# Products of 512 columns in place of two of 256 in some steps of a gated-linear-attention block

## The chip, the cores and the metric

The kernel runs on one core of one Trainium2 chip. The metric is device time in microseconds of one execution, taken as the median over several runs. A profile is one further execution, recorded by the hardware profiler; its span goes from the first to the last instruction of the program, and its own time is a little longer than that.

The core has a matrix engine (TensorE, in the profile PE; its loads of the stationary operand are listed apart as PEld), a vector engine (VectorE, DVE), a scalar engine (ScalarE, ACT), GpSimd (POOL) and SyncE (SP), which issues most of the DMAs. TensorE reads its operands from on-chip memory (SBUF) and adds its products into eight banks of accumulators (PSUM), each of 128 partitions by 512 float32.

## The reference

One layer of a hybrid encoder: 256 tokens, width 2048, depth 1, so that the only mixer is gated linear attention (GLA), followed by a squared-ReLU MLP and a final normalization. Everything is float32.

```python
def reference(x, ...):
    h = x
    h = h + _gla_mixer(_rmsnorm(h, gla_norm), gla_w_in, gla_w_gate_up, gla_b_gate, gla_o_norm, gla_w_out)
    h = h + _sq_relu_mlp(_rmsnorm(h, mlp_norm), mlp_w_up, mlp_w_down)
    return _rmsnorm(h, final_norm)

def _gla_mixer(h, w_in, w_gate_up, b_gate, o_norm, w_out):
    q, k, v, r, g_low = split(h @ w_in)          # 1024, 1024, 2048, 2048, 16 columns
    log_a = log_sigmoid(g_low @ w_gate_up + b_gate) / 16
    # four heads, chunks of 64 tokens: a decayed state per head, read by q
    ...
    return (normalized(o) * silu(r)) @ w_out

def _sq_relu_mlp(h, w_up, w_down):               # 2048 -> 8192 -> 2048
    a = relu(h @ w_up)
    return (a * a) @ w_down
```

## The kernel before

**Precision.** Each float32 matrix is split into a high and a low part that the matrix engine takes in one pass each (type `F32R`): `hi` is a rounded copy, made by ScalarE (line 109), `lo` the difference, made by VectorE (line 110). A product of two matrices A and B is three products: high by high, high by low, low by high. A weight tile of 128 rows and up to 1040 columns is loaded into `raw` by SyncE's DMA queue (line 132, function `weights`) and then split into a slot of the rings `hi` and `lo`, five slots each. `raw` has three buffers, each of which holds two tiles.

**The two forms of a projection.** In `natural` the tokens are the stationary operand, in blocks of 128 tokens by 128 inputs, and the weight columns move through TensorE; the output has tokens on partitions. It makes 16 steps over the 2048 inputs (`kt`). In each step there are two token blocks `t`, three terms, and the parts of the output's columns given by `cuts`; `HALF` is two parts of 512, each one PSUM bank. The part of 512 columns is issued by the helper `halves` (line 140) as products of `T` = 256 columns each, with the same stationary operand, one after the other. A width that isn't a multiple of 256 is issued whole: the first stage has a part of 272 columns, that is three products of 256 and one of 272 for each token block and term. In `turned` (line 169) the weights are the stationary operand and the 256 tokens move, so that each product has 256 columns.

**Stages, in order.** First half of the values with the gate's low-rank input (`w_vg`); keys and queries (`turned`, two halves of 512 outputs each); second half of the values (`3 * KEYW`, with the steps in the order `late`); two gate projections (`4 * KEYW` and `5 * KEYW`, 1024 columns each), after each of which `gate_out` applies the SiLU and multiplies with the attention's output; two output projections (`w_out`, 1024 columns each) with the attention's output, transposed, as the stationary operand (`row_o`); then four rounds of the MLP, each of four `up` passes (`turned`, 512 hidden units each) and a `down` pass for each half of the output's columns. The last half of the last round is written out apart, with the final normalization.

**The down pass.** `down(r, half, act)` makes an output of 256 tokens by 1024 columns from 2048 hidden units. For the first 512 of its columns it uses a Strassen-like scheme over pairs of steps (banks `b32`, `b74`, `b16`, `b50`; combined weights are made by VectorE in `work`). The other 512 columns, the plain half, are ordinary products: `blocks`, for both token blocks and three terms, into the two banks `plain`. In the first pair of steps (`PLAIN`) everything is ordinary.

**Addresses.** The stationary operands of the projections lie at chosen places of SBUF. The normalized input `xth`, `xtl` has rows of 320 elements at an offset of 48; for step `EVEN` = 5 a copy in the tile `xe` is used instead. The output projection's operand (`row_o`, line 528) has the offset 48 before step 5, 64 at step 5, and 112 after it. In `turned` the weight slots have the offset 48, or 0 in the steps that `even` names.

**Order of the work.** Small pieces of other work wait in the list `side` and are issued by `pump`, one after each step: scores, attention (`attend`, itself with products of 256 columns through `halves`), transposes (`turn`, line 515), sums of squares. The order on each engine is then settled by a planner that simulates a timeline as the program is built; so products of neighbouring steps and of side work can be found interleaved in the trace. TensorE's queue carries nothing but products and transposes.

Of the kernel before, what the change touches and what calls it, by code (L numbers as in the profile page):

```python
# [34 lines left out]
NT = T // P  # L35
D = 2048
KT = D // P
# [3 lines left out]
KEYW = HEADS * DK  # L41
# [5 lines left out]
G = 1024  # L47
# [19 lines left out]
def tile_gla_mlp(ctx, tc, x, xt, cols, w_vg, w_in, w_gate, w_out, w_up, w_down, final_norm, out):  # L67
    nc = tc.nc
# [10 lines left out]
    def acc_banks(n):  # L79
        return [acc_p.tile([P, 512], F32, tag="acc", name="acc") for _ in range(n)]  # L80
# [7 lines left out]
    def pump(n=1):  # L88

        with tc.issue_after(last_hi[0].ins), tc.issue_after(last_lo[0].ins):  # L90
            for _ in range(n):
                if side:
                    side.popleft()()

    def flush():
        while side:
            side.popleft()()
# [4 lines left out]
    def slots(off=0):  # L102
        return [wpool.tile([P, SLOT], F32R, tag=i, name=i)[:, off:] for i in ("hi", "lo")]

    def parts(raw, n, to, pieces=None):

        hi, lo = to
        for s in (slice(*p) for p in pieces or [(0, n)]):
            last_hi[0] = nc.scalar.copy(hi[:, s], raw[:, s])  # L109
            last_lo[0] = nc.vector.tensor_tensor(lo[:, s], raw[:, s], hi[:, s].bitcast(F32), op=ALU.subtract)  # L110
        return hi, lo
# [3 lines left out]
    def raw_pair():  # L115
        a = wpool.tile([P, 2 * WMAX], F32, tag="raw", name="raw", bufs=3)
        return a[:, :WMAX], a[:, WMAX:]

    def weights(src, n, pieces=None, room=None, skip=0, raw=None, off=0):

        to = room or slots(off)
        if raw is None:
            if not raw_half:
                raw_half.extend(raw_pair())
            raw = raw_half.pop(0)
        for s in (slice(*p) for p in pieces or [(0, n)]):
            dst = raw[:, s]
            if len(src.shape) == 3:
                dst = dst.rearrange("p (i c) -> p i c", i=2)
                last_load[0] = nc.sync.dma_start(out=dst, in_=src)  # L130
            else:
                last_load[0] = nc.sync.dma_start(out=dst, in_=src[:, s])  # L132
        return parts(raw, n, to, pieces or [(skip, n)])

    def halves(o, x, w, first, last):

        n = w.shape[-1]
        for c in range(0, n, T) if n % T == 0 else (0,):
            m = slice(c, c + T) if n % T == 0 else slice(0, n)
            nc.tensor.matmul(o[:, m], x, w[:, m], start=first and c == 0, stop=last, skip_group_check=True)  # L140

    def natural(row, source, n, cuts, pumps=1, ahead=None, order=range(KT)):

        acc = acc_banks(NT * len(cuts))
        acc = [acc[t * len(cuts) : (t + 1) * len(cuts)] for t in range(NT)]
        for step, kt in enumerate(order):
            wh, wl = weights(source(kt), n, ahead and ahead(kt))
            for t in range(NT):
                sh, sl = (a[:, t * P : (t + 1) * P] for a in row(kt))
                for i, (s, w) in enumerate(((sh, wh), (sh, wl), (sl, wh))):  # L150
                    for c, (lo, hi) in enumerate(cuts):
                        halves(acc[t][c], s, w[:, lo:hi], step == 0 and i == 0, step == KT - 1 and i == 2)
            if step < KT - 1:
                pump(pumps)
        return acc
# [21 lines left out]
    HALF = [(0, 512), (512, 1024)]  # L177

    def rows(w, c0, n=G, r0=0):
        return lambda kt: w[r0 + kt * P : r0 + (kt + 1) * P, c0 : c0 + n]  # L180
# [50 lines left out]
    cuts = [(0, 512), (512, 768), (768, WMAX)]  # L231
# [80 lines left out]
    acc = natural(row_x, rows(w_vg, 0, WMAX), WMAX, cuts, ahead=input_tile)  # L312
# [92 lines left out]
    for half in range(2):  # L405
        acc = turned(*xts, w_in, KEYW + half * GT, even=(0,) if half else (2,))
# [18 lines left out]
    for half in range(2):  # L425
        acc = turned(*xts, w_in, half * GT, even=())
# [6 lines left out]
    at = big.tile([P, 2, HEADS, 3 * P + 64], F32R, tag="C", name="at")  # L433
# [36 lines left out]
    acc = natural(row_x, rows(w_in, 3 * KEYW), G, HALF, order=late)  # L470
# [49 lines left out]
            nc.scalar.activation(dh, s, AF.Copy, scale=gain(kt))  # L520
            nc.vector.scalar_tensor_tensor(dl, s, gain(kt), dh.bitcast(F32), op0=ALU.mult, op1=ALU.subtract)

    acc = natural(row_x, rows(w_in, 4 * KEYW), G, HALF)
    flush()
    gate_out(acc, 0)
    oth, otl = (big.tile([P, KT * T + 128], F32R, tag="B", name="ot" + i) for i in "hl")
# [7 lines left out]
    acc = natural(row_x, rows(w_in, 5 * KEYW), G, HALF)  # L534
# [20 lines left out]
    acc = natural(row_o, rows(w_out, 0), G, HALF)  # L555
# [3 lines left out]
    row_h = lambda kt: [a[:, kt, :] for a in (hth, htl)]  # L559
    side.extend([lambda: None] + [lambda q=q: turn(h, row_h, g2, q) for q in range(4)])  # L560
    side.append(lambda: ssq_h(0))
    acc = natural(row_o, rows(w_out, G), G, HALF)
    flush()
    add_h(acc, G)
    side.extend([lambda q=q: turn(h, row_h, g2, q) for q in range(4, 8)])
# [24 lines left out]
    A11, A12, A21, A22, S3, S1, S2, S4 = range(8)  # L590
# [35 lines left out]
    def down(r, half, act):  # L626

        c0 = half * G
        plain = [aux_bank(), aux_bank()] if half == 0 else acc_banks(2)
        b32, b74 = acc_banks(2) if half == 0 else [aux_bank(), aux_bank()]  # L630
        b16, b50 = acc_banks(2)
        left, right = slice(0, T), slice(T, 2 * T)
        used = set()

        def product(bank, o, a, w, m, last):

            for i, (x, y) in enumerate(((0, 0), (0, 1), (1, 0))):
                halves(bank[:, o], a[x], w[y][:, m], bank.name not in used, last and i == 2)
                used.add(bank.name)

        for kp in range(KP):
            last = kp == KP - 1
            at = lambda f: stationary(act, kp, f)
            w = rows(w_down, c0, G, r * D)
            blocks = lambda i, wi: [
                product(plain[t], slice(0, 512), at((A11, A21)[t] + i), wi, slice(512, G), last and i == 1) for t in range(NT)
            ]
            if kp in PLAIN:
                for i in range(2):
                    wi = weights(w(2 * kp + i), G)  # L650
                    blocks(i, wi)
                    product(b32, slice(0, 512), at(A11 + i), wi, slice(0, 512), False)
                    product(b50, right, at(A21 + i), wi, left, False)
                    product(b74, right, at(A21 + i), wi, right, False)
                    pump()
                continue
            assert not raw_half
            pair = wpool.tile([P, 2 * WMAX], F32, tag="raw", name="raw", bufs=3)
            raw0, raw1 = pair[:, :WMAX], pair[:, WMAX:]
            w0 = weights(w(2 * kp), G, skip=T, raw=raw0)  # L660
            product(b16, left, at(A11), w0, right, last)
            blocks(0, w0)
            pump()
            w1 = weights(w(2 * kp + 1), G, raw=raw1)
            u = work[:, kp % 2].rearrange("p (f s) -> p f s", f=4)
            add = lambda o, x, y: nc.vector.tensor_tensor(o, x, y, op=ALU.add)

            both = pair[:, T : T + 2 * (WMAX - T)].rearrange("p (k c) -> p k c", k=2)[:, :, :T]
            add(u[:, :2], raw0[:, left].unsqueeze(1).to_broadcast([P, 2, T]), both)
            add(u[:, 2], u[:, 0], raw1[:, left])  # L670
            add(u[:, 3], u[:, 2], raw1[:, right])
            wu = parts(work[:, kp % 2], G, slots())
            product(b32, right, at(A12), w1, right, last)
            product(b32, left, at(S4), w1, left, last)
            blocks(1, w1)
            product(b50, left, at(S1), wu, slice(0, T), last)
            product(b74, left, at(S3), wu, slice(T, 2 * T), last)
            product(b16, right, at(S2), wu, slice(2 * T, 3 * T), last)
            product(b74, right, at(A22), wu, slice(3 * T, G), last)
            if not last:  # L680
                pump()
        flush()
        for t in range(NT):
            take(plain[t], t, c0 + 512, 512)

        tt = lambda o, x, y: nc.vector.tensor_tensor(o, x, y, op=ALU.subtract)
        nc.scalar.copy(ends[:, 1], b16[:, left])
        tt(ends[:, 3], ends[:, 1], b16[:, right])
        tt(ends[:, 0], b50[:, left], ends[:, 3])
        tt(ends[:, 2], ends[:, 3], b74[:, left])  # L690
        take(b32, 0, c0, 512)
        take(b74, 1, c0, 512)
        take(b50[:, right], 1, c0, T)
        for t in range(NT):
            hv = h[:, t, c0 : c0 + 512].rearrange("p (i s) -> p i s", i=2)
            nc.vector.tensor_tensor(hv, hv, ends[:, 0 : t + 2 : t + 1], op=ALU.add)
# [23 lines left out]
    cuts = [HALF, [(0, 512), (512, 768), (768, 1024)]]  # L720
    acc = [acc_banks(len(cuts[t])) for t in range(NT)]
# [10 lines left out]
    for kt in range(KT):  # L732
        k = kt - KT + ROOM
        w = weights(rows(w_down, G, G, (ROUNDS - 1) * D)(kt), G, room=k >= 0 and [room[:, i, k, :] for i in range(2)])
# [68 lines left out]
```

## Time and profile before

| | us |
|---|---|
| Median of 3 runs | 1075.46 (1075.1 to 1075.59) |
| Profiled execution, its own time | 1075.4 |
| Span of the profiled execution | 1073.3 |
| TensorE busy in it | 1063.1 |
| VectorE busy | 774.9 |
| ScalarE busy | 573.7 |

A busy time is the union of an engine's instructions. TensorE's products overlap each other: a product of 256 columns is listed with some 277 ns, but the next one starts while it still runs. So what counts for TensorE is the distance from one start to the next, which is read from the chain in order of time (a start, a length, the engine, the tile and the line, and the number of products) or from the timeline (a start, a duration, the engine, the line, what is written from what, the shape, and the number of instructions merged). In both, "acc<-hi,xh" names the output, the moving operand and the stationary operand. A table by stretches gives, for each, the stretch, its length, then the busy time and number of instructions for PE, PEld, DVE, ACT and POOL, the granted TensorE clock, the DMA share and GB/s.

The steps that the change touches run at these times of the profiled execution: the first gate projection's steps 6 to 15 at 214 to 244 us, the second output projection's steps 5 to 15 at 351.8 to 382 us, and the two down passes of round 1 at 641.8 to 724 us.

### The profile page before, as it was taken

The page shows a single profiled execution, that of the slowest core. Times are in us where ns is not written, and L with a number is a line of the kernel's source. Part 1 is how long each engine was busy: PE and PEld are TensorE (multiplying, and loading weights), DVE is VectorE, ACT ScalarE, POOL GpSimd, SP SyncE. Part 2 cuts the span into 40 slices and gives each one's busy share as a digit, 9 for nine tenths or more (in the row PEclk, how much of TensorE's full clock was granted, in tenths as well). Part 3 has the DMA queues.
Part 4 walks back from the last instruction along what each step waited for, and adds up shares of the span by engine and source line. Part 5 has one row for each costly group of instructions (what it writes and reads, how often), then busy time and mean ns, then how long its engine had stood idle before and what let it go on. Part 6 is the DMA issues. An engine that isn't in the chain of part 4 may idle for free.

```text
span 1073.3 us, 21863 instructions
## 1 busy us (share of the span) xinstructions
PE 1063.1 (99%) x9285; PEld 1062.3 (99%) x9285; DVE 774.9 (72%) x1027; ACT 573.7 (53%) x694; POOL 12.7 (1%) x39
## 2 busy tenths in 40 slices
PE   9999999999999999999999999999999999999997
PEld 9999999999999999999999999999999999999997
DVE  6668644556555466789986679986779997678874
ACT  6675444546444454556554456564555554555552
POOL 0000000000000000000000000000000000000000
PEclk9999999999999999999999999999999999999999
DMA  9856664556545555556566555566654666655662
GB/s 328 313 174 201 196 190 144 166 153 193 196 164 191 196 163 192 196 174 217 199 212 206 188 195 183 197 212 221 197 197 167 218 205 209 192 196 188 206 230 79
DMA packets 81009, 210.43 MB, mean 196 GB/s; under 512 B 6752, under 2 KB 9824, under 8 KB 80784
## 3 DMA queue, kind: packets, MB, share of 16 engines
q1 hardware_dynamic: 79808, 206.86, 58.4%
q10 hardware_dynamic: 1104, 2.19, 0.5%
q8 instruction: 72, 1.18, 0.4%
q14 instruction: 25, 0.20, 0.1%
HBM read 206.92 MB, written 2.10 MB: 195 GB/s over the span
## 4 chain that ended last, share of the span: by engine, by line
PE 98%; issue 1%; DMA 0%; DVE 0%; ACT 0%; SPq 0%; POOLq 0%; POOL 0%; DVEq 0%; ACTq 0%
PE acc L140 43%; PE acc L169 41%; PE aux L140 12%; PE aux L515 1%; PE aux L442 1%; DMA raw<-in_w_vg 0%; PE aux L343 0%; SPq L132 0%; DVE vl L307 0%; DVE hf L762 0%; ACT sqf L715 0%; DVE h L622 0%; ACT vh L306 0%; ACT hi L109 0%; POOLq L799 0%
## 5 line engine op out<-in xcount | busy, mean ns | idle before, releaser
L110 DVE TENSOR_TENSOR lo<-raw,hi 128x1024 fp32r<-128x1024 f32 (+3 forms) x386 | 454.3, 1178 | 242.4 <-ACT hi L109 241.2
L109 ACT CAST hi<-raw 128x1024 fp32r<-128x1024 f32 (+3 forms) x386 | 391.2, 1015 | 404.9 <-PE acc L169 175.4
L169 PE MATMUL acc<-hh,hi 128*128 128x256 f32 x1024 | 283.3, 277 | 0.0
L169 PE MATMUL acc<-hh,lo 128*128 128x256 f32 x1024 | 283.2, 277 | 0.0
L169 PE MATMUL acc<-hl,hi 128*128 128x256 f32 x1024 | 283.1, 276 | 0.0
L140 PE MATMUL acc<-hi,act 128*128 128x256 f32 x1202 | 217.3, 276 | 0.0
L169 PEld LDWEIGHTS acc<-hh,lo 128*128 128x128 f32 x1024 | 192.4, 188 | 0.0
L169 PEld LDWEIGHTS acc<-hh,hi 128*128 128x128 f32 x1024 | 192.4, 188 | 0.0
L169 PEld LDWEIGHTS acc<-hl,hi 128*128 128x128 f32 x1024 | 192.4, 188 | 0.0
L140 PEld LDWEIGHTS acc<-hi,act 128*128 128x128 f32 x1202 | 180.3, 188 | 0.0
L140 PE MATMUL acc<-lo,act 128*128 128x256 f32 x601 | 142.1, 276 | 0.0
L140 PE MATMUL aux<-hi,act 128*128 128x256 f32 x716 | 135.1, 276 | 0.0
L140 PEld LDWEIGHTS aux<-hi,act 128*128 128x128 f32 x716 | 107.9, 188 | 0.0
L140 PEld LDWEIGHTS acc<-lo,act 128*128 128x128 f32 x601 | 101.9, 188 | 0.0
L140 PE MATMUL acc<-lo,xh 128*128 128x256 f32 x480 | 77.5, 279 | 0.0
L140 PE MATMUL aux<-lo,act 128*128 128x256 f32 x358 | 76.9, 276 | 0.0
L140 PE MATMUL acc<-hi,xh 128*128 128x256 f32 x480 | 75.8, 280 | 1.0 <-ACT hi L109 1.0
L140 PE MATMUL acc<-hi,xl 128*128 128x256 f32 x480 | 76.6, 279 | 0.0
L169 PE MATMUL acc<-xh,hi 128*128 128x256 f32 x256 | 70.9, 277 | 0.4 <-DVE vl L307 0.4
L169 PE MATMUL acc<-xl,hi 128*128 128x256 f32 x256 | 71.0, 277 | 0.0
L169 PE MATMUL acc<-xh,lo 128*128 128x256 f32 x256 | 70.8, 277 | 0.0
L109 ACT CAST hi<-work 128x1024 fp32r<-128x1024 f32 x49 | 51.7, 1056 | 31.4 <-PE aux L140 12.0
(137 smaller groups left out, 1249.9 us busy)
## 6 DMA issues: line engine op xcount, KB each, us to landing
raw<-in_w_up SPq DMA_DIRECT2D x128, 512.0 KB, 4.5
raw<-in_w_down SPq DMA_DIRECT2D x128, 512.0 KB, 4.3
raw<-in_w_in SPq DMA_DIRECT2D x80, 512.0 KB, 4.7
raw<-in_w_out SPq DMA_DIRECT2D x32, 512.0 KB, 4.3
raw<-in_w_vg SPq DMA_DIRECT2D x13, 520.0 KB, 8.4
h<-in_x SPq DMA_DIRECT2D x4, 512.0 KB, 7.3
zz<-in_xt SPq DMA_DIRECT2D x2, 512.0 KB, 9.9
fb<-in_final_norm ACTq DMA_DIRECT2D x1, 1024.0 KB, 6.7
```

Source lines behind the costliest of these rows:

```text
L109: last_hi[0] = nc.scalar.copy(hi[:, s], raw[:, s])
L110: last_lo[0] = nc.vector.tensor_tensor(lo[:, s], raw[:, s], hi[:, s].bitcast(F32), op=ALU.subtract)
L140: nc.tensor.matmul(o[:, m], x, w[:, m], start=first and c == 0, stop=last, skip_group_check=True)
L169: nc.tensor.matmul(o, u[:, s], m[:, kt], start=kt == 0 and n == 0 and j % 2 == 0, stop=kt == KT - 1 and n == 2, skip_group_check=True,)
L442: nc.tensor.matmul(o, kab[:, k[0], c0 + c, k[1] : k[1] + P], q(qt[:, c0 + c]), start=c == 0, stop=c == 1)
L515: nc.tensor.transpose(b[:, i * T + t * P : i * T + (t + 1) * P], src[:, t, kt * P : (kt + 1) * P], ident)
```

## The change

`halves` gets a switch, `whole`. While it is on, a part is issued as one product over all its columns, instead of one for each 256 columns. `natural` takes a list of steps, `by_512`, and turns the switch on for the products of these steps, and off before the side work of the step is issued. Two of the projections are given such a list: the first gate projection, steps 6 to 15, and the second output projection, steps 5 to 15. In the down passes `blocks`, the plain half, turns it on in round 1, in both halves of the output. In all of them the parts are 512 columns wide, so each such product fills one PSUM bank. The operands, their places, the order of terms and the accumulation are the same.

```diff
+    whole = [False]
+
     def halves(o, x, w, first, last):
 
         n = w.shape[-1]
+        if whole[0]:
+            nc.tensor.matmul(o, x, w, start=first, stop=last, skip_group_check=True)
+            return
         for c in range(0, n, T) if n % T == 0 else (0,):
...
-    def natural(row, source, n, cuts, pumps=1, ahead=None, order=range(KT)):
+    def natural(row, source, n, cuts, pumps=1, ahead=None, order=range(KT), by_512=()):
...
         for step, kt in enumerate(order):
+            whole[0] = step in by_512
...
+            whole[0] = False
             if step < KT - 1:
                 pump(pumps)
...
-    acc = natural(row_x, rows(w_in, 4 * KEYW), G, HALF)
+    acc = natural(row_x, rows(w_in, 4 * KEYW), G, HALF, by_512=range(6, KT))
...
-    acc = natural(row_o, rows(w_out, G), G, HALF)
+    acc = natural(row_o, rows(w_out, G), G, HALF, by_512=range(5, KT))
...
-            blocks = lambda i, wi: [
-                product(plain[t], slice(0, 512), at((A11, A21)[t] + i), wi, slice(512, G), last and i == 1) for t in range(NT)
-            ]
+            def blocks(i, wi):
+                whole[0] = r == 1
+                for t in range(NT):
+                    product(plain[t], slice(0, 512), at((A11, A21)[t] + i), wi, slice(512, G), last and i == 1)
+                whole[0] = False
+
```

## The prediction

> **What bounds the kernel.** I read the page first (busy times, clock, chain), then the waits, then the chain in order of time through the stages that the change touches, last the timeline of TensorE where products start unusually far apart.
>
> ```profile
> PE 1063.1 (99%) x9285; PEld 1062.3 (99%) x9285; DVE 774.9 (72%) x1027; ACT 573.7 (53%) x694; POOL 12.7 (1%) x39
> PEclk9999999999999999999999999999999999999999
> PE 98%; issue 1%; DMA 0%; DVE 0%; ACT 0%; SPq 0%; POOLq 0%; POOL 0%; DVEq 0%; ACTq 0%
> ```
>
> TensorE is the chain: 98% of it, at full clock. The waits say the same:
>
> ```profile
> ACT hi L109 <- PE acc L140: 144.6, 127, 2.9
> PE aux L195 <- DVE ones L192: 1.0, 1, 1.0
> PE acc L140 <- ACT hi L109: 1.0, 1, 1.0
> ```
>
> ScalarE, which makes the `hi` half of each weight tile, waits for TensorE to free a slot (127 times); TensorE waits for ScalarE once. So the time is the number of products times their distance from start to start. A busy figure of 99% can't give that distance; the chain in order of time can, since it gives a stretch's length and its number of products:
>
> ```profile
> 203.69 2.83 PE acc L140 x24
> ...
> 215.01 2.72 PE acc L140 x24
> ...
> 226.57 24.48 PE acc L140 x216
> ```
>
> 24.48 us over 216 products is 113.3 ns; 2.72 over 24 the same; but at 203.69 it is 2.83 over 24, 117.9 ns, for the same shapes. And the step whose stationary operand lies in `xe` is at 120 ns (8 products from 212.25 to 213.21):
>
> ```profile
> 212.25 1.12 PE L140 MATMUL acc<-hi,xe 128*128 128x256 f32 x8
> 213.21 0.64 PE L140 MATMUL acc<-lo,xe 128*128 128x256 f32 x4
> ```
>
> The reader should see three regimes of one instruction: 113.3, 117.8 and 120.0 ns. Going through the starts of all products: 117.8 comes after score products or transposes and stays (159.9 to 211, 293 to 300, 342 to 352, 384 to 401 us); 120 appears where the stationary operand has the offset that `xe`, or `row_o` at kt 5, or `off=0` gives it; and after each of those steps 113.3 is back. The first stage, with its 272-column products, never gets to 113.3:
>
> ```profile
> 28.22 0.64 PE L140 MATMUL acc<-hi,xh 128*128 128x256 f32 x4
> 28.70 0.64 PE L140 MATMUL acc<-lo,xh 128*128 128x256 f32 x4
> ```
>
> That is 480 ns for 3 x 256 + 272 columns. There, the next start comes 124.5 ns after a 272 and 117.8 on average after a 256: 6.7 ns for 16 columns, 0.417 ns a column. So 256 columns are 106.7 ns, and what is left over per product is 6.7 ns at 113.3, 11.1 at 117.8 and 13.3 at 120.
>
> **The change, part by part.**
>
> *Products replaced.* Gate projection, steps 6 to 15: 10 steps x 2 token blocks x 3 terms x 2 banks = 120 products of 512 for 240 of 256. Second output projection, steps 5 to 15: 11 x 12 = 132 for 264. Down passes of round 1: 16 steps x 2 x 3 = 96 in each half, 192 for 384. Together 444 products and 444 weight loads fewer; columns stay. In the trace these are at 214 to 244, 351.8 to 382 and 641.8 to 724 us, and all of them run at 113.3 today except step 5 of the output projection, at 120.
>
> *Price of one product of 512.* The trace has none, so it is bounded. Columns: 512 x 0.417 = 213.3 ns. The leftover, from the nearest rows: 6.7 (state of the stages in question) to 13.3 (`xe` row), once per product, so 220.0 to 226.7. From below: the score products of 192 columns, which stream longer than a weight load takes, start 162.5 ns apart; their columns cost about twice as much (51.5 ns for the 64 columns between 128 and 192), and two column times each, 160 ns, leave 2.5. That gives 215.8. From above: if the leftover is a share of the columns rather than a fixed amount, 512 costs two of 256: 226.7, in the worst row 240. The 272 row speaks for a fixed amount: 16 more columns add exactly their column time. I take 220.0, since it is the row of the same operation, addresses and stages; 215.8 and 240 are kept for the range.
>
> *Sum.* 432 merges at 2 x 113.3 - 220.0 = 6.67 ns: 2.88 us. The 12 of step 5 at 2 x 120 - 226.7 = 13.3 ns: 0.16 us. Together 3.0 us, all on the chain, as nothing else holds it. 1.3 us of this is in the down passes, 0.8 and 0.9 in the two projections.
>
> *What must keep up.* Feeding: a projection step shrinks from 2.72 to 2.64 us, against ScalarE 1.05 and VectorE 1.23 us for its weight tile and 512 KB from memory (198 GB/s, where the first slice of the page moves 328). The tightest place is the down passes:
>
> ```profile
> 641.00:722.00 81.00, 81.00 (x717) 81.00 (x717) 74.94 (x102) 47.92 (x50) 0.00 (x0) 1.00 0.57 196
> ```
>
> VectorE has 74.9 of 81.0 us (third pair); TensorE would need 79.7, at 215.8 per product 78.9. The cover thins from 6.1 to 4.8 or 4.0 us but stays, so it costs nothing; were it gone, the two passes could not fall below 75. No wait, DMA or bank moves: a bank is still released after its last product, a weight slot after the last product that reads it; nothing on SyncE's or GpSimd's queue is passed. The planner orders side work by its own estimate and may shift transposes a little; what hangs on it is how long a 117.8 stretch after them lasts. The one that follows the output projection (384 to 401 us) costs 17 us x 4.4 / 117.8 = 0.6 us, so I put 0.7 either way for this and nothing in the sum.
>
> The profiled execution took 1075.4 us (span 1073.3), the median of the runs is 1075.46: 1075.4 - 3.0 = 1072.4.
>
> **The rivals.**
>
> *The weight load was the limit, and hides now (faster still).* Each weight load starts 3 ns after the product before it and its product 110 ns later, in every 113.3 stretch. If that wait, not the stream, makes the 6.7, a stream of 213 ns covers it and 2.5 is left, as in the score row. Saved: 444 x 10.8 = 4.8 us, time 1070.6. Against it: the 272 products stream 6.7 ns longer and keep their whole leftover.
>
> The Trainium skill, page "TensorE: Matmul & The Clock Gate", section "Back-to-back issue gap", gives warm products columns / 2.4 + 2.5 ns, which is 215.7 for 512, and so this rival's time. By the same rule 256 columns would take 109.2 where the trace has 113.3, so on these operands it is off today; for 512 no run has shown it yet.
>
> *Mixed widths bring the 117.8 state.* The one stage that mixes widths never reaches 113.3 though it has an `xe` step, so products of 512 may do the same to themselves and to the 256s between them. The 432 then save 2.2 each (0.97), step 5 saves 12 x 15.6 = 0.19; the 342 products of 256 in the two down passes cost 4.4 more (1.51), the remaining attention products 0.16, and the first five steps of the next gate pass, up to their `xe` step, 0.53. Net +1.0, time 1076.4. For it: the 272 stage. Against it: there the odd width returns every fourth product, while in the projections the 512s stand together.
>
> *The leftover grows with the columns (slower).* If it comes from the two operand streams meeting in memory (the `xe` rows show that the stationary operand's place alone moves a product from 113.3 to 120), a stream twice as long can meet twice as often, and 512 costs what two of the worst row do, 240 ns: 432 x 13.3 = +5.8, time 1081.2. It ends slower from 231.5 ns a product (444 x 4.85 = 2.15 us). For it: address dependence. Against: a product of 512 brings one weight load, not two, and the 272 row.
>
> *Nothing in time.* 226.7 a product, everything else as before: 1075.4.
>
> **How the numbers follow.** Forecast 0.42 (1072.4, itself 1071.7 to 1073.2 with the planner's 0.7); weight load 0.18 (1070.6); mixed widths 0.18 (1075.0 to 1079, as the 256s go to 117.8 or to 120; with 120 and no saving it is 342 x 6.7 + 0.8 = +3.1); growth 0.18 (1078 to 1081); nothing 0.04. About 0.2%, 2.15 us, is what a measurement tells from no change. Faster: 0.42 + 0.18 + 0.02 of the mixed case = 0.62. Same: 0.10 of the mixed case and 0.04 = 0.14. Slower: 0.06 + 0.18 = 0.24. A range from 1070.2 to 1077.8 leaves out the growth case, the worst of the mixed case and a tail below: about 0.2.
>
> **What would show it.** Right: 444 products of 128x512 in the groups, 8841 TensorE instructions, 24.48-us stretches of 216 products becoming 108 of them in 23.8 us; the 256s of the down passes still at 113.3; VectorE's idle time in 641 to 722 down by about a microsecond. The first rival: 23.3 us for that stretch. The second: 256s at 117.8 between the 512s and after 244 us. The third: 512 starts 230 ns or more apart. The forecast would be wrong above all if the leftover isn't fixed, or if the state after a 512 is another than 113.3.

## The result, and the profile after

| | before | after |
|---|---|---|
| Median | 1075.25 us of 7 runs (1074.88 to 1075.59) | 1078.72 us of 7 runs (1077.12 to 1080.06) |
| Ratio, after by before | | 1.0026, 95% interval 1.0017 to 1.0035 |
| Profiled execution, own time | 1075.4 | 1077.12 |
| Its span | 1073.3 | 1075.1 |

The changed kernel is slower, by about a quarter of a per cent, where 1072.4 was forecast. Its profiled execution is the lowest of its seven, so the two traces differ by 1.8 us where the medians differ by 3.5. Three of the seven runs, 1079.2 to 1080.06 us, list a mean granted clock of 0.996 or 0.997, the other four, with a median of 1077.7, one of 0.998 or 0.999. A second measurement of the same kernel (below) gave 1077.72.

The page of the changed kernel: busy times of the engines, TensorE's granted clock, and the shares of the chain that ended last.

```profile
PE 1065.6 (99%) x8841; PEld 1046.2 (97%) x8841; DVE 775.3 (72%) x1027; ACT 573.5 (53%) x694; POOL 12.7 (1%) x39
PEclk9999999999999999999999999999999999999999
PE 98%; issue 1%; DMA 0%; DVE 0%; ACT 0%; POOLq 0%; POOL 0%; DVEq 0%; SPq 0%; ACTq 0%
```

444 instructions of TensorE are gone, as counted, at the same full clock, and TensorE is still 98% of the chain. Fewer products, all of the same engine, took longer. The waits of the changed kernel, TensorE's own (waiting instruction, what it waits for, us in total, times, longest):

```profile
PE aux L202 <- DVE ones L199: 1.0, 1, 1.0
PE acc L176 <- DVE vl L314: 0.4, 1, 0.4
PE acc L145 <- ACT hi L109: 0.3, 1, 0.3
```

No new wait. The two down passes by stretches, first of the kernel before, then of the changed one:

```profile
641.90:683.10 41.20, 41.20 (x366) 41.20 (x366) 38.07 (x53) 25.91 (x28) 0.00 (x0) 1.00 0.55 189
683.10:724.20 41.10, 41.10 (x365) 41.10 (x364) 38.17 (x52) 23.25 (x25) 0.00 (x0) 1.00 0.62 204
```

```profile
642.60:684.40 41.80, 41.80 (x268) 37.76 (x267) 38.15 (x53) 25.79 (x28) 0.00 (x0) 1.00 0.55 186
684.40:726.10 41.70, 41.70 (x271) 37.70 (x270) 38.30 (x52) 23.29 (x25) 0.00 (x0) 1.00 0.61 201
```

TensorE is busy for the whole of each stretch in both; VectorE (third pair) has 38.15 and 38.30 us of 41.8 and 41.7, so about 3.5 us a pass are left in which it isn't needed: this is its cover. The passes are longer because the products are further apart. (Each stretch is cut at a round tenth; measured to the product, the passes are 0.77 and 0.40 us longer.)

The distance of the products is read from the chain in order of time (start, length, tile, line, number of products). In the changed kernel L141 is a product of 512 columns, L145 one of 256, L522 a transpose. The gate projection:

```profile
213.86 0.68 PE aux L145 x6
214.54 3.20 PE acc L141 x14
217.75 1.41 PE aux L145 x12
219.16 2.30 PE acc L141 x10
221.46 0.68 PE aux L145 x6
222.14 3.66 PE acc L141 x16
225.80 1.41 PE aux L145 x12
227.22 18.31 PE acc L141 x80
...
250.98 0.44 PE aux L522 x4
```

The stretch of 80 is 18.31 us: 228.9 ns a product. Two of 256 took 226.7 there before. Single starts go 226, 229, 232, 226, 229, 232 ns, a cycle of three. The attention's products between (aux) are at 113.3 ns in the groups of 6 and at 117.5 in the two groups of 12. From the first of these rows to the transposes it is 37.12 us; the same work before took from 214.33 to 251.06, 36.73. The difference, 0.39, is 120 x 2.3 = 0.28 for the products of 512 and 24 x 4.4 = 0.11 for the attention's.

The first down pass of the changed kernel, where something turns:

```profile
655.64 1.37 PE aux L141 x6
657.02 1.70 PE acc L145 x15
658.72 1.37 PE aux L141 x6
660.09 0.11 PE acc L145
660.20 0.46 PE aux L141 x2
660.66 0.59 PE acc L145 x5
661.25 0.92 PE aux L141 x4
662.16 1.77 PE acc L145 x15
```

Up to 660 the groups are the ones of the kernel before: six products of 512, then 15 or 6 of 256 at 113.3 ns (1.70 / 15). At 660.09 one product of 256 has slipped in among a group of 512s, which becomes 2 and 4; from there to the end of the pass the 256s are at 118 (0.59 / 5, 1.77 / 15). Before the change the same groups read 1.70 for 15 and 0.68 for 6 throughout:

```profile
656.28 1.70 PE acc L140 x15
...
659.34 0.68 PE acc L140 x6
```

The output projection and the stretch behind it, of the changed kernel, and of the kernel before behind the projection (L169 there is L176 here, products of 256 with turned weights):

```profile
353.11 29.76 PE acc L141 x130
...
401.86 10.23 PE acc L176 x87
```

```profile
398.66 13.35 PE acc L169 x115
```

130 products at 228.9 again. Behind it the 256s come at 117.6 where they came at 116.1: in the kernel before they returned to 113.3 at 401, behind a first group at 120 ns; in the changed one that group leaves them at 117.8, and they return at 410.4, behind the next one.

To account for the whole, I compared the times at which the same number of columns has passed TensorE in both traces:

| stretch (time in the trace of before) | after minus before, us |
|---|---|
| up to 30 us (first loads) | -0.47 |
| gate projection, 214 to 250 | +0.39 |
| transposes and steps at 250 to 262 | +0.30 |
| output projection, 352 to 382 | +0.15 |
| next pass, 382 to 412 | +0.27 |
| down passes, first half of the output | +0.77 |
| down passes, second half | +0.40 |
| everything else | 0.00 |

The sum is 1.81, the difference of the spans. From 30 us on it is +2.28.

The +0.30 at 250 to 262 is a change of state too. Products and transposes stand there in the same order in both traces; the 72 products of 256 between the transposes run at 117.8 now, and ran at 113.3 before (72 x 4.4 = 0.32). One group of 24, first before, then after:

```profile
251.49 2.73 PE acc L140 x24
```

```profile
251.41 2.83 PE acc L145 x24
```

### The profile page after: what moved, and what is told of

It is laid out like the page before. It is cut to its first block, busy times and chain, and to the rows that moved or that the text cites. A ratio compares the mean times of both kernels' runs of the same rounds, so it can differ in the third digit from the quotient of the medians.

```text
span 1075.1 us, 20976 instructions
## 1 busy us (share of the span) xinstructions
PE 1065.6 (99%) x8841; PEld 1046.2 (97%) x8841; DVE 775.3 (72%) x1027; ACT 573.5 (53%) x694; POOL 12.7 (1%) x39
## 4 chain that ended last, share of the span: by engine, by line
PE 98%; issue 1%; DMA 0%; DVE 0%; ACT 0%; POOLq 0%; POOL 0%; DVEq 0%; SPq 0%; ACTq 0%
PE acc L176 41%; PE acc L145 36%; PE aux L145 10%; PE acc L141 7%; PE aux L141 2%; PE aux L522 1%; PE aux L449 1%; DMA raw<-in_w_vg 0%; PE aux L350 0%; DVE vl L314 0%; DVE hf L772 0%; ACT sqf L725 0%; DVE h L629 0%; ACT vh L313 0%; POOLq L809 0%
## 5 line engine op out<-in xcount | busy, mean ns | idle before, releaser
L176 PE MATMUL acc<-hh,hi 128*128 128x256 f32 x1024 | 283.3, 277 | 0.0
L176 PE MATMUL acc<-hl,hi 128*128 128x256 f32 x1024 | 283.2, 277 | 0.0
L176 PE MATMUL acc<-hh,lo 128*128 128x256 f32 x1024 | 283.1, 276 | 0.0
L145 PE MATMUL acc<-hi,act 128*128 128x256 f32 x1074 | 198.1, 276 | 0.0
L176 PEld LDWEIGHTS acc<-hh,hi 128*128 128x128 f32 x1024 | 192.4, 188 | 0.0
L176 PEld LDWEIGHTS acc<-hl,hi 128*128 128x128 f32 x1024 | 192.4, 188 | 0.0
L176 PEld LDWEIGHTS acc<-hh,lo 128*128 128x128 f32 x1024 | 192.4, 188 | 0.0
L145 PEld LDWEIGHTS acc<-hi,act 128*128 128x128 f32 x1074 | 163.6, 188 | 1.1
L145 PE MATMUL acc<-lo,act 128*128 128x256 f32 x537 | 129.8, 276 | 0.0
L145 PE MATMUL aux<-hi,act 128*128 128x256 f32 x588 | 112.8, 276 | 0.0
L145 PEld LDWEIGHTS acc<-lo,act 128*128 128x128 f32 x537 | 92.3, 188 | 0.9
L145 PEld LDWEIGHTS aux<-hi,act 128*128 128x128 f32 x588 | 89.8, 188 | 0.6
L176 PE MATMUL acc<-xh,hi 128*128 128x256 f32 x256 | 70.9, 277 | 0.4 <-DVE vl L314 0.4
L176 PE MATMUL acc<-xl,hi 128*128 128x256 f32 x256 | 71.0, 277 | 0.0
L176 PE MATMUL acc<-xh,lo 128*128 128x256 f32 x256 | 70.8, 277 | 0.0
L110 DVE TENSOR_TENSOR lo<-work,hi 128x1024 fp32r<-128x1024 f32 x49 | 59.9, 1222 | 7.5 <-ACT hi L109 6.1
L145 PE MATMUL acc<-lo,xh 128*128 128x256 f32 (+1 forms) x400 | 65.1, 280 | 0.1
L145 PE MATMUL aux<-lo,act 128*128 128x256 f32 x294 | 64.5, 276 | 0.0
L145 PE MATMUL acc<-hi,xl 128*128 128x256 f32 (+1 forms) x400 | 64.2, 279 | 0.0
```

The lines of the kernel that those rows point to most:

```text
L176: nc.tensor.matmul(o, u[:, s], m[:, kt], start=kt == 0 and n == 0 and j % 2 == 0, stop=kt == KT - 1 and n == 2, skip_group_check=True,)
```

## The experiments

Four causes were to be told apart: the price of a product of 512 by itself (theory 1: about 229 ns whatever else); a lost cover of VectorE in the down passes (theory 2); the places of the two operands in memory (theory 3); and the state in which the 256s are left. The number that the expectations give a later theory is told where it comes up. Diffs are against the changed kernel.

**Each part alone.** Three kernels, each with one of the changed parts.

Gate projection alone:

```diff
-    acc = natural(row_o, rows(w_out, G), G, HALF, by_512=range(5, KT))
+    acc = natural(row_o, rows(w_out, G), G, HALF)
...
-                whole[0] = r == 1
+                whole[0] = False
```

> Only the gate projection's steps 6 to 15 are issued as 512 columns. Theory 1 (a product of 512 has a fixed price of 228.9 ns, 15.6 over its columns, and afterwards the 256s run at 113.3 or 117.8 according to where in a repeating pattern they come in): 120 x 2.2 = 0.27 us for the products, 0.1 to 0.2 for attention products at 117.8 between them, 0.2 to 0.5 for the next gate pass up to its xe step: +0.5 to +0.9 us against before. Theory 2 (products of 512 cost nothing by themselves, the loss in the changed kernel comes from the down passes, where VectorE is nearly full): 0 within 0.2 us, and 512s at 226.7 or less.

Output projection alone:

```diff
-    acc = natural(row_x, rows(w_in, 4 * KEYW), G, HALF, by_512=range(6, KT))
+    acc = natural(row_x, rows(w_in, 4 * KEYW), G, HALF)
...
-                whole[0] = r == 1
+                whole[0] = False
```

> Only the second output projection's steps 5 to 15. Theory 1: 120 products at +2.2 ns are +0.27 us, the 12 of step 5 at 240 - 229 save 0.13, and the up pass after it stays at 117.8 up to its own reset, which is the case before as well: -0.1 to +0.5 us. Theory 2: 0 within 0.2 us.

Down passes alone:

```diff
-    acc = natural(row_x, rows(w_in, 4 * KEYW), G, HALF, by_512=range(6, KT))
+    acc = natural(row_x, rows(w_in, 4 * KEYW), G, HALF)
...
-    acc = natural(row_o, rows(w_out, G), G, HALF, by_512=range(5, KT))
+    acc = natural(row_o, rows(w_out, G), G, HALF)
```

> Only the plain half of the two down passes of round 1. Theory 1: 192 x 2.2 = 0.43 us, and between 0 and 342 x 4.4 = 1.5 us for the 256s between them, by the share of them at 117.8: +0.4 to +1.9 us, with a spread from run to run that the kernel before doesn't have, and no idle time of TensorE. Theory 2 (VectorE is late): gaps in TensorE's work, starts of products over 240 ns after a wait for lo, VectorE busy over 78 us of the 84 us of the passes.

| | median of 11 | before, 27 runs | ratio, 95% | in the trace, from 30 us on |
|---|---|---|---|---|
| gate alone | 1076.01 | 1075.34 | 1.0008 (0.9999 to 1.0016) | +0.69 |
| output alone | 1076.05 | 1075.34 | 1.0006 (0.9997 to 1.0015) | +0.15, behind it +0.27, and +0.30 at 250 to 262 |
| down alone | 1076.80 | 1075.34 | 1.0010 (1.0001 to 1.0019) | +1.17 |

The medians add to 0.67 + 0.71 + 1.46 = 2.8 us; each part loses, none alone beyond what a median can tell with certainty except the down passes. The traces are sharper. Each part shows the same stretch changed by the same amount as in the whole change, so the parts don't act on each other. One term can't be put down to the products of 512: the kernel with the output projection alone has the +0.30 at 250 to 262 as well, ahead of anything that it changes, while the one with the down passes alone has nothing there. With it, this kernel is slower by more than the +0.5 that was the most expected of theory 1. What makes the transposes at 251 leave one state or the other isn't shown. The output projection of its kernel, by the chain:

```profile
354.85 27.47 PE acc L141 x120
```

228.9 ns. For theory 2, the two down passes of the kernel with them alone, as one stretch:

```profile
643.60:726.90 83.30, 83.30 (x535) 75.26 (x534) 76.27 (x104) 48.97 (x52) 0.00 (x0) 1.00 0.58 193
```

VectorE is busy for 76.27 of 83.30 us and TensorE waits nowhere in them; before, VectorE had 76.24 in 82.3. Theory 2 falls.

**What a product costs by itself.** TensorE issues rows of 36 equal products with nothing beside them (one execution, as with the other kernels of products alone below). The place of the stationary and of the moving operand changes by row, between rows stand 12 products with both operands at equal places; the widths, and what stands ahead of a row, change too.

```diff
+    def product(n, so, mo):
+        k = count[0]
+        count[0] += 1
+        s = (k // 2) % 3 * 256 + so
+        m = k % 2 * 1024 + mo
+        nc.tensor.matmul(banks[k % 4][:, :n], st[:, s : s + P], mv[:, m : m + n], start=True, stop=True, skip_group_check=True)
...
+    for n in (256, 512):
+        for so in (0, 16, 32, 48):
+            for mo in (0, 16, 32, 48):
+                for _ in range(12):
+                    product(256, 0, 0)
+                for _ in range(36):
+                    product(n, so, mo)
```

> Nothing but products in long rows: no projection, no attention and no MLP is computed, the output is the last four banks. Rows of 36 products with 256 or 512 columns, the stationary operand at 0, 64, 128 or 192 bytes past a multiple of 256, the moving operand likewise, each after a row of 12 products in the place of the xe step; then offsets of 16 bytes, widths from 272 to 480, rows after float32 products, and rows of 13 to 18 products of 512 followed by 24 of 256. Theory 1: 512 is 228.9 in every place, 256 is 113.3 or 120.0 by the place, and 256s after 512s are at 113.3 or 117.8 by the number of 512s before them. Theory 3 (the leftover of a product comes from the two streams meeting in memory, so it goes with the places): 512 differs by place by 7 ns or more, with 220 in the best.

Below, a place is the byte offset of an operand modulo 256, stationary / moving; the offsets 48 and 112 of the kernel (float32) are 192, the weights that move are at 0. The distance of the products in ns, without the first six of a row, and behind it what is left over the columns at 0.417 ns:

| place (stationary / moving) | 256 columns | 512 columns |
|---|---|---|
| equal (four of them) | 120.0 (13.3) | 226.7 (13.3); 227.1 at 64/64 |
| 192/0, the kernel's | 113.3 (6.7) | 228.8 (15.5) |
| 0/192, 128/64 | 113.3 (6.7) | 233.2, 233.3 (20) |
| 64/128, 128/192 | 117.8 (11.1) | 228.9, 229.0 (15.6) |
| 64/0, 0/64, 192/128 | 117.8 (11.1) | 233.2 to 233.4 (20) |
| 128 apart (four) | 118.7 to 118.8 (12.1) | 232.2 to 233.5 (19 to 20) |

Rows of its trace, by the chain, each from within one row of the table: 256 columns at 0/0, at 192/0 and at 192/64, then 512 at 0/0, 192/0 and 0/64.

```profile
16.89 5.16 PE acc L88 x43
86.98 2.61 PE acc L88 x23
92.55 2.73 PE acc L88 x23
109.52 6.80 PE acc L88 x30
226.69 6.64 PE acc L88 x29
119.14 7.00 PE acc L88 x30
```

That is 120.0, 113.5, 118.7, 226.7, 229.0 and 233.3 ns. Theory 1 in its strict form falls, since the price of a 512 goes with the place; what theory 3 had right is that, what it had wrong is the best value: no product of 512 came below 226.7. So the kernel's two products of 256 at 113.3 cost exactly what the best product of 512 does.

The other widths, at 192/0, show which row is the odd one. 272 columns took 126.6 ns, 320 took 146.7, 384 took 173.3, 448 took 200.0: 13.3 left over each time (288 had 11.7, 480 had 18.2). The leftover of 6.7 belongs to 256 columns alone, at three of the sixteen places and at one of six between them that the same kernel runs, 192/48. This one is also among the best for 512; there, 256 and 512 columns by the chain:

```profile
294.43 2.38 PE acc L88 x21
347.89 6.80 PE acc L88 x30
```

That is 113.3 and 226.7 ns: two small products and one large cost the same.

The Trainium skill, page "TensorE: Matmul & The Clock Gate", section "Step-by-step: what each phase is for", says that the load of the next stationary operand takes no read bandwidth from the product that runs. The table bears on it, but doesn't settle it: moving the stationary operand alone, with the moving one at 0, takes a product of 256 from 113.3 to 120.0 and one of 512 from 226.7 to 233.2. Whether that is bandwidth, or why else the place matters, isn't shown by any run.

The rows behind float32 products began and stayed at 117.8 for 256 columns at 192/0, three times of three; 512 columns there were at 228.9, 233.3 and 228.8. So that place has two states, for either width.

The last rows of this kernel have 12 products of 256 at 0/0, then 13 to 18 of 512 at 192/0, then 24 of 256 at 192/0. Theory 1 let these go by the number of 512s. They are at 117.8 behind all six; here behind 15 and behind 18:

```profile
466.77 2.24 PE acc L88 x19
...
491.10 2.24 PE acc L88 x19
```

**What sets the state, first try.** Products alone again. Behind 6 float32 products and 12 of 256 at 192/0, or behind 12 products of 512, come r products of 256 at 0/0 and then 30 of 256 at 192/0; then, behind 24 products of 256 at 0/0, 6 or 12 products of 512 in turn with 18 of 256 at 192/0, the 512s first at 192/0, then at 0/0; then one product of 272 among 256s.

```diff
+    for r in (0, 1, 2, 4, 8, 12):
+        for _ in range(12):
+            product(512, 48, 0)
+        for _ in range(r):
+            product(256, 0, 0)
+        for _ in range(30):
+            product(256, 48, 0)
...
+    for _ in range(3):
+        for _ in range(24):
+            product(256, 0, 0)
+        for _ in range(36):
+            product(256, 48, 0)
+        product(272, 48, 0)
+        for _ in range(36):
+            product(256, 48, 0)
```

> Rows of products alone, as before, nothing of the layer is computed: after float32 products, 12 products of 256, then 0 to 24 products of 256 in the place of the xe step, then 30 of 256 in the place of the others; the same after 12 products of 512; then 6 or 12 products of 512 in turn with 18 of 256, the 512s in the one place and in the other; then single products of 272 among 256s. Theory 1: 256s after 512s at 117.8, back at 113.3 only after a number of 120-ns products, and a single 272 among 256s at 113.3 suffices for 117.8. Theory 5 (a 512 doesn't touch the state; what puts the 256s to 117.8 is side work): 113.3 throughout after 512s.

Of nine counts of 0/0 products behind float32, only 8 brought 113.3 back; of six behind the 512s, only 1. So products like those of the `xe` step don't bring 113.3 back reliably. 6 or 12 products of 512 at 192/0, first behind the 24 at 0/0 and then behind 256s at 113.3, left the 256s at 113.3 in six rows of six, so theory 1, which had 117.8 behind any 512s, doesn't hold; the same numbers of 512s at 0/0 left them at 117.8 in six of six, so theory 5, that a 512 doesn't touch the state, falls too. And a single 272 turned 113.3 into 117.8, three times of three; ahead of it and behind it, by the chain:

```profile
185.85 3.85 PE acc L88 x34
...
190.05 3.77 PE acc L88 x32
```

113.2 and 117.8 ns. One product of another width is enough, and the 256s behind it don't recover by themselves.

**The count of the 512s.** In the gate projection the four groups of 512s leave 14, 24, 40 and 120 issued; the 256s behind 24 and 120 are at 113.3, those behind 14 and 40 at 117.5. As the starts of the 512s go in a cycle of three, the theory (the sixth) was that the state left behind goes by their count modulo three. Products alone: 18 of 256 at 192/0, a products of 512, 18 of 256, 12 - a of 512, 18 of 256, for a from 0 to 12.

```diff
+    for a in range(13):
...
+        for _ in range(a):
+            product(512, 48, 0)
+        for _ in range(18):
+            product(256, 48, 0)
+        for _ in range(12 - a):
+            product(512, 48, 0)
```

> Rows of products alone, nothing of the layer is computed. From 18 products of 256 at 113.3 ns, a products of 512, 18 of 256, 12 - a of 512, 18 of 256, for a from 0 to 12. Theory 6 (the 512s run in a cycle of three starts, 226, 229 and 232, and the 256s come back at 113.3 only if the cycle is complete): 113.3 after a = 0, 3, 6, 9, 12 and 117.8 after the other eight. Theory 1 in its loose form (by chance): no order in a.

The 256s behind a products of 512, by the chain, for a = 1, 3 and 5:

```profile
33.46 1.88 PE acc L88 x16
...
57.59 1.81 PE acc L88 x16
...
81.61 1.89 PE acc L88 x16
```

117.5, 113.1 and 118.1 ns. Over all a: 113.3 for 0, 3, 6 and 9, 117.8 for 1, 2, 4, 5, 7, 8, 10 and 11. (The row of a = 12 was at 117.8 ahead of its first 512.) So from the state of 113.3 the rule of three holds. The way back is another matter: after the remaining 12 - a it was 113.3 again in all but a = 11, but in the down pass above the 256s stay at 118 behind further groups of six.

The starts in the traces show what the count stands for: the point of the cycle at which the 512s end. In the changed kernel 37 groups of 512s are followed by five or more products of 256. Where the last 512 has 231 or 232 ns to the next start, the 256s are at 113.3 (21 groups); where it has 225 to 230, they are at 117.8 (16 groups). The groups of six that keep the slow state begin with 233 or 234 and end with 229 or 230, so they come into the cycle at another point and leave it before 232. In the 24 groups of the rows by count it is the same (14 at 231 or 232, 10 at others, one of them at 233), and the six rows of 13 to 18 end at 225, 226 or 229.

**Another place.** Both output projections with products of 512 from step 5 on, and their stationary operand at the offset 64 (place 0/0) in all those steps; nothing else of the change.

```diff
-        c = kt * T + (OFF if kt < EVEN else 64 if kt == EVEN else OFF + 64)
+        c = kt * T + (OFF if kt < EVEN else 64)
...
-    acc = natural(row_o, rows(w_out, 0), G, HALF)
+    acc = natural(row_o, rows(w_out, 0), G, HALF, by_512=range(5, KT))
```

> Both output projections, steps 5 to 15, with products of 512, and row_o from step 5 on at the offset 64 (same place as the moving operand, modulo 256 bytes) in place of 112 after step 5. Theory 3 (the place sets the leftover): 226.7 ns a product instead of 228.9, so 240 products at no cost, step 5 saves 12 x 13.3 = 0.16 us in each pass: -0.3 us against before, plus up to 0.6 us for 256s at 117.8 after the two passes. Theory 1 in its strict form (228.9 in every place): +0.2 us for the products, plus the same 0.6.

1075.59 us against 1075.32 (ratio 1.0004, 0.9995 to 1.0013). The last ten steps of both projections, by the chain:

```profile
308.98 27.20 PE acc L141 x120
...
354.83 27.20 PE acc L141 x120
```

226.7 ns, where the kernel with the output projection alone had 27.47 for the same 120. Place accounts for this part of the loss, in the kernel as in the rows of products. The stretch behind the projection is 0.27 longer all the same, with the 512s at 226.7 as at 228.9: it isn't their price that does that, but the state they leave, as in the rows with 512s at 0/0.

**The same kernel again**, unaltered, to see which losses are fixed.

> The changed kernel once more, unaltered, for a second trace on the chip of the others. If the losses are fixed by place and order: the same 0.5 us in the gate projection, 0.1 in the output projection, 1.2 in the down passes as in the first trace, and a difference in the start before 30 us. If the state is by chance of the run: the down passes anywhere from 0.4 to 1.9 us.

1077.72 us (11 runs) against 1075.32 (27): ratio 1.0024, 1.0015 to 1.0033. The trace is the first one's, stretch by stretch: +0.39, +0.30, +0.15, +0.27, +0.77, +0.39. The stretch up to 30 us is -0.14 where it was -0.47. Over all traces of these kernels it lies between -0.8 and +1.6, with the first loads; that is what varies between the two traces, and the rest is the same in both.

**Where the 256s are slow.** If 512s cost 229 and 256s cost 120 or 117.8 in some stages, the 512s belong there. First a wide version: both value stages in all steps, the gate projection's first five steps, the second output projection's steps 1 to 4, and none of the changed parts.

```diff
-    acc = natural(row_x, rows(w_vg, 0, WMAX), WMAX, cuts, ahead=input_tile)
+    acc = natural(row_x, rows(w_vg, 0, WMAX), WMAX, cuts, ahead=input_tile, by_512=range(KT))
...
-    acc = natural(row_x, rows(w_in, 3 * KEYW), G, HALF, order=late)
+    acc = natural(row_x, rows(w_in, 3 * KEYW), G, HALF, order=late, by_512=range(KT))
...
-    acc = natural(row_x, rows(w_in, 4 * KEYW), G, HALF, by_512=range(6, KT))
+    acc = natural(row_x, rows(w_in, 4 * KEYW), G, HALF, by_512=range(5))
...
-    acc = natural(row_o, rows(w_out, G), G, HALF, by_512=range(5, KT))
+    acc = natural(row_o, rows(w_out, G), G, HALF, by_512=range(1, 5))
```

> The products of 512 are put where 256s run at 117.8 to 120 today, and nowhere else: the first part of the value stage with the 272s (all steps), the second value stage (all steps), the gate projection's steps 0 to 4 (its xe step stays at 256 and resets), the second output projection's steps 1 to 4. Theory 1 (a 512 costs 226.7 to 229 here whatever the state before it): 96 x 7 = 0.7 us, 192 x 6.7 = 1.3, 60 x 6.7 = 0.4, 48 x 6.7 = 0.3, together 2.7 us less than before, 1072.6. Theory 4 (a 512 takes the state of its surroundings, and is worse where they are slow): 0 to 2 us more than before.

1075.15 us against 1075.32: ratio 1.0000, 0.9991 to 1.0009, where theory 1 had 2.7 us less. Theory 4, that a 512 takes the state of its surroundings, allowed 0 to 2 more. By the trace the kernel won 0.54 in the first value stage, 1.05 at 159 to 213 us (at 183 to 195 with its 512s at 233, still under two of 256 at 117.8) and 0.4 in the output projection's first steps. It gave back about as much: +0.15 at 143 to 159, where the 256s had been at 113.3; +0.23 at 250 to 262, as in other kernels; and +1.3 in the output projection's later steps, whose 256s were now left at 117.8:

```profile
354.82 28.74 PE acc L145 x244
```

28.74 / 244 is 117.8 ns. Step 5, behind which they had been at 113.3 before, did not bring them back.

Then only stages that had won: the first value stage in all steps, the second in its steps 6 to 11 (counted from 0), the gate projection's first five; down passes and output projections without 512s.

```diff
-                order=late, by_512=range(KT))
+                order=late, by_512=range(6, 12))
...
-    acc = natural(row_o, rows(w_out, G), G, HALF, by_512=range(1, 5))
+    acc = natural(row_o, rows(w_out, G), G, HALF)
```

(This diff is against the wide version.)

> As the run with 512s in the slow places, without what lost there: the second value stage has them in its steps 6 to 11 alone (from the score products on, up to its xe step), the second output projection has none. By the stages of that run's trace: 0.55 us less in the first value stage, 1.0 to 1.2 less in the second, 0.2 less in the gate projection's first five steps, nothing lost behind: 1.7 to 2.0 us less after the start, 1073.3 to 1073.8 in the median. If 512s leave a worse state behind them also here: 0 to 1 less.

1073.55 us (11 runs, 1073.28 to 1074.34) against 1075.32 (15 runs): ratio 0.9984, 0.9975 to 0.9993. This beats both kernels. Its first value stage and its second, by the chain:

```profile
9.84 40.77 PE acc L141 x258
...
159.09 5.72 PE acc L141 x25
```

Before, the first read

```profile
9.99 41.54 PE acc L140 x346
```

By three products (512, 256 and 272 columns) it is 474.1 ns in place of 480.2 by four; and 228.8 for a 512 in the second, where two of 256 in the state of 117.8 cost 235.6. Stretch by stretch its trace has -0.5 in the first stage, -1.0 at 159 to 212 and +0.22 at 250 to 262, together -1.3 where 1.7 to 2.0 less was expected. A further -0.5 of the span's difference lies in the first loads and isn't claimed for the edit; that the median falls within what was expected may be luck.

## Why the prediction was wrong

**The step that failed is "Price of one product of 512".** It took the leftover, 6.7 ns, as a fixed amount per product, "the row of the same operation, addresses and stages", and added the columns. The leftover isn't fixed. It measured 15.6 at those places, so a product costs 228.9 to 229.8, not 220.0. The 432 products then don't save 2.88 us: with 229.0 in the gate, 228.9 in the output projection and 229.6 in the down passes they cost 0.28 + 0.27 + 0.57 = 1.12 more than the pairs. That step alone is 4.0 of the 5.3 us between the forecast of -3.0 and the +2.28 of the trace.

**The row that misled was the 272.** Its 16 more columns added exactly their column time, and this was read as proof of a fixed leftover. But it was read against 256s of the same stage, which the 272 itself keeps out of 113.3. Alone and against 113.3, a 272 takes 126.6: 13.3 more, of which 6.7 are columns. At these places no width other than 256 had less than 11.7 left over. A difference between two rows shows a fixed amount only if both rows are in the state that is wanted.

**The first rival** (the weight load hides, 215.8) is out: the weight load has a stream twice as long to hide behind and the leftover is larger. So is the rule beside it, from the Trainium skill's page "TensorE: Matmul & The Clock Gate", section "Back-to-back issue gap", 215.7 ns for 512, which the page gives for an isolated product: these operands, in a stream, measured 226.7 to 233.5, and the measurement decides.

**The second rival** (mixed widths bring 117.8) had the mechanism that the forecast lacked, in weaker form. The 726 products of 256 in the down passes were all at 113.3 before; in the changed kernel 101 of 171 in the first half and 28 of 171 in the second were at 116 or more, about 0.47 + 0.13 = 0.6 us (171 x 2.7 and 171 x 0.8 ns), with 0.11 in the attention's products. The rival gave the whole 1.51 for the down passes, and credited the 512s with a saving of 2.2 each that they cost instead; its 1076.4 is the nearest of the numbers by a coincidence of these two. What it missed is the rule: it isn't mixing as such, but a group of 512s that ends before its cycle of three is complete.

**The third rival** (the leftover grows with the columns) was right that it grows, 6.7 to 15.6, and that it hangs on addresses; its size, 240, was the worst row doubled. Its own limit, slower from 231.5 by more than 0.2%, wasn't reached by the 512s (228.9 to 229.8); the rest came from the 256s.

**The other steps.** The twelve products of step 5 were right in sign: their starts settle at 226 to 227 as foreseen, less a slow first few behind the transposes, and save about 0.12 against 0.16. Feeding and cover held: no wait, and VectorE inside its passes. The 0.7 put either way for the state behind transposes covers the 0.27 behind the output projection and the 0.30 at 250 to 262, but its reason doesn't: in the second, products and transposes kept their order and left another state. That TensorE's starts set the time, that 8841 instructions would be left and that nothing else holds the chain was right. The terms together: 1.12 - 0.12 + 0.11 + 0.6 + 0.27 + 0.30 = 2.28, what the trace has from 30 us on.

**What stays open.** The 3.5 us between the first medians hold 1.2 more than the trace accounts for; the four runs named with them have 2.4, as has the second measurement, and that fits the trace. Why +0.30 appears at 250 to 262 isn't shown, nor what in the hardware keeps the state. A version of the change whose groups of 512s end on a complete cycle wasn't tried; by the traces it could win back the 0.7 of the 256s but not the price of the 512s.

## What to carry to other kernels

A width that the trace doesn't hold has no price yet: a row of products of that width, at the very places of the kernel's operands, settles in one run what a sum of columns and a leftover got wrong by 9 ns a product. Before merging products, ask which state the small ones are in: two of 256 at 113.3 equal the best 512 (226.7), and only where they run at 117.8 or 120 can the 512 win. Where products of several widths share a queue, look at those behind the odd one, since a single product can slow those that follow.

## What the runs showed of the hardware

- The distance of products of one width goes with the places of both operands modulo 256 bytes: 113.3 to 120.0 ns for 256 columns, 226.7 to 233.5 for 512. Of the sixteen places at multiples of 64 bytes none is best for both; at 192/48 both are at their best.
- At one and the same place, 256 columns have two states, 113.3 and 117.8. One 272 leaves the slower one (three of three), float32 products alone do too (twelve rows of twelve; the transposes at 251 us left it in one trace and not in another), and so do 512s at 192/0 unless their last start is 231 or 232 ns ahead of the next; from the state of 113.3 that is a count that is a multiple of three. The 256s run on in it, for 244 products in the output projection above.
- 512s at 192/0 start 226, 229 and 232 ns apart in a cycle of three; at 0/0 they keep 226.7.
